# A two-layer diffusion trunk on one core: the first scale vector by column blocks, and the first two feed-forward products row tile by row tile

## The chip, the cores and the metric

The kernel runs on one core of a Trainium2 chip, as one program in one launch. The metric is the device time of that launch in microseconds (us). The core has five engines that run side by side, each through its own instructions in order: TensorE (matmuls; in the profile PE, and PEld for its weight loads), VectorE (DVE), ScalarE (ACT), GpSimd (POOL) and SyncE (SP), which here issues transfers. The transfers themselves run on 16 DMA engines.

## What is computed

Two layers of a backbone over 512 latent tokens and 256 context tokens of width 1024. Each layer is a half-step SwiGLU, a mixer, and a second half-step SwiGLU. Only the very start matters here: the modulation of layer 0 and the first feed-forward block.

```python
def adaln(cond, prm):
    mod = jax.nn.silu(cond) @ prm["mod_w"] + prm["mod_b"]
    return jnp.split(mod, N_MOD, axis=-1)
def half_ffn(x, m, name):
    sh, sc, g = m
    h = modulate(rms_norm(x, prm[name + "_norm"]), sh, sc)
    return x + 0.5 * g * swiglu(h, prm[name + "_w_in"], prm[name + "_w_out"])
```

The modulation is made for two conditions, one for the latent tokens and one for the context tokens. Of the nine chunks of 1024 entries, chunk 0 is the shift and chunk 1 the scale of the first feed-forward block.

## The kernel before

Tokens lie along the free axis: the input x is eight row tiles of 128 features by 768 tokens (`xv[d]`, tiles A, two to a buffer). The gain of the norm and the scale are multiplied to one factor per feature (`am`), the norm's reciprocal per token (`rb`) is applied behind the product, and the shift goes through the weights as extra columns. So the first products need `am` and x, but neither the norm nor the shift.

**A product** (`product(u)`) takes one unit of the input weights, 128 x 1024 values loaded by SP into a buffer `r` of two. ACT copies it in a rounded form (`wh`, L210) and DVE subtracts that from the original (`wl`, L211); tiles of x are split likewise into B (ACT, L386) and C (DVE, L387) by `prep(d)`. For each of the eight row tiles k three pairs of matmuls follow (`wh` with B, `wh` with C, `wl` with B), a pair being 512 and 256 tokens (helper line L190). Products are summed in PSUM in tiles `pa` (two) and `pb` (one). The first three products are "late" ones: the shift's columns come behind them, as 48 matmuls of 4 or 2 columns (`shifts`), once the shift is known.

**The scale and the shift** come from `mod_unit`: a unit is 128 rows of the modulation's weights by 1024 columns (512 KB), loaded by SP, and four fp32 matmuls of 256 columns in four strips of the array (L305; the trace counts each fp32 matmul as two). Eight units make a chunk, which two matmuls (L193) and DVE then bring into columns. At the start eight units run for the scale, through two buffers `m` and the two buffers `r`; a unit's load waits for the matmuls that used its buffer. Then SP loads the x tiles and the first two weight units, and `set_am` makes `am`. The eight units for the shift (`fill`) stand between the matmuls of products 1 and 2, one at every second row tile, through the two buffers `m`.

**Around it.** `sq_acc` squares the tiles of x on ACT (L374, L377) and sums them on POOL (L196); six matmuls with the sum as weights (L269, one column each), a chain on DVE and ACT, and two broadcast matmuls (L279) make `rb` during product 2 (`rb_steps`).

The order on each engine is set by a scheduler from the order of the code; instructions handed to `pin` keep their place. Buffers come from rings, and an instruction waits until the one that used its buffer last is done.

Of the kernel before, what the change touches and what calls it, by code (L numbers as in the profile page):

```python
# [8 lines left out]
F32 = mybir.dt.float32  # L9
F32R = mybir.dt.float32r  # L10
AF = mybir.ActivationFunctionType
ALU = mybir.AluOpType
# [7 lines left out]
NT = NL + NC  # L20
# [34 lines left out]
HD = 0  # L55
NLATE = 3
# [7 lines left out]
RAWD = (0, 5)  # L64
# [9 lines left out]
def _cols():  # L74
    if _COLS:
        return _COLS
    off = 0
    for name, n in (
        ("modb0", 72), ("modb1", 72), ("nrm0", 24), ("nrm1", 24), ("sel", 8),
        ("kvg", 2), ("qg", 3), ("gq96", 1), ("gk96", 1), ("glub", 8), ("dw", 124), ("dwb", 4),  # L80
        ("lng", 4), ("lnb", 4), ("gkr", 32), ("gqr", 32),
        ("gqq", 64), ("gqk", 64),
        ("ident", 128),
    ):
        _COLS[name] = (off, n)
        off += n
    _COLS["_n"] = (off, 0)
    return _COLS


class Kern:
    def __init__(self, tc, es, ins, out, dbg=None):
# [12 lines left out]
        const = pool("const", 1)  # L105
# [16 lines left out]
        nc.scalar.dma_start(self.small, ins["small"])  # L122
# [12 lines left out]
        nc.vector.tensor_copy(self.identr, self.col("ident"))  # L135
# [5 lines left out]
    def col(self, name):  # L141
        o, n = _cols()[name]
        return self.small[:, o:o + n]
# [149 lines left out]
    def mod_unit(self, both=False):  # L293
# [5 lines left out]
        if both and k % 2:  # L299
            u = self.wr.tile([128, 1024], F32, name=self.nm("r"), tag="r")  # L300
        else:
            u = self.mr.tile([128, 1024], F32, name=self.nm("m"), tag="m")
# [12 lines left out]
        for b in range(2):  # L315
# [4 lines left out]
                mb.unsqueeze(3).broadcast_to((128, 2, 4, 2)), ALU.add)  # L320

# [87 lines left out]
    def ffn(self, win, wout, lat_only, after, mid=None, late=None, fill=(), raws=(), split=None):  # L409
# [25 lines left out]
        def product(u):  # L435
            w = self.unit(win[u], 1024, self.pin if u < n_late else lambda i: i, raws.pop(0) if raws else None)
# [62 lines left out]
        u = j = 0  # L499
        for ci, n in enumerate(CHUNKS):  # L500
# [849 lines left out]
    def build(self):  # L1350
# [20 lines left out]
        for L in range(2):  # L1371
# [31 lines left out]
            first = dict(late=(lambda d: self.prep(d, False, self.pin), lambda d: self.sq_acc(d, NT, 0, self.pin), shift0), raws=raws, fill=[lambda: self.mod_unit(False)] * 8) if L == 0 else {}  # L1403
# [111 lines left out]
def layout(a):  # L1515
    a = {k: np.asarray(v) for k, v in a.items()}
    r = {}
# [6 lines left out]
    r["modw0"] = np.ascontiguousarray(a["l0_mod_w"][:, :2048])  # L1524
# [94 lines left out]
```

## Time and profile before

| what | before |
|---|---|
| median of three runs | 2865.4 us (2865.26 to 2869.09) |
| the profiled execution | 2866.9 us, of which the span is 2865.0 us |
| TensorE busy | 2792.8 us |
| VectorE, ScalarE, GpSimd busy | 1588.1, 858.3, 317.0 us |
| first product's first matmul | 22.87 us |
| first matmul behind the shift's columns | 72.85 us |

The page gives busy times by engine, and the chain of work that ended last, followed back from the end. The timeline shows each engine's instructions with start, duration and, in brackets, the idle time just before and what ended it; starts that follow each other closely are the better measure of a matmul's cost, since the durations overlap. The windows view gives busy time, the granted TensorE clock (1.00 is 2.4 GHz, 0.50 is 1.2 GHz) and the transfers' share in chosen stretches. The granted clock is printed as 1.00 until its first record, at 29.36 us here; before that the distance of the matmuls tells the pace.

### The profile page before, as it was taken

To read this page: it belongs to the slowest core of one execution; us is meant where nothing else is said; L and a number is where in the kernel's file an instruction comes from. 1 tells how busy PE (TensorE), PEld (TensorE's weight loads), DVE (VectorE), ACT (ScalarE), POOL (GpSimd) and SP (SyncE) were. 2 spreads that over 40 slices of the span, in tenths; PEclk is the share of its full clock that TensorE was granted. 3 is DMA by queue.
4 is the path that set the end of the run, shared out by engine and by line. 5 is a ranking of instruction groups with operands and counts; after the bars stand their busy time and mean duration, and the time that the engine had idled before them with its cause. 6 is when DMAs were issued, how large, how long until landed. Compare 5 with 4: busy or idle time off the path is not lost.

```text
span 2865.0 us, 41335 instructions
## 1 busy us (share of the span) xinstructions
PE 2792.8 (97%) x17180; PEld 2429.3 (85%) x17180; DVE 1588.1 (55%) x2618; ACT 858.3 (30%) x1284; POOL 317.0 (11%) x357
## 2 busy tenths in 40 slices
PE   7999999999978999999999999999999999999999
PEld 5888888887767788888888888888887878898998
DVE  2674675678565576747535432333347689644443
ACT  3221212242456422122122221221224267322222
POOL 1000000030022320000002100000021156300000
PEclk9999999999989999999999999999999999999999
DMA  6343343442200224426411121212133200322232
GB/s 234 126 149 109 116 156 104 133 138 75 72 30 20 63 95 130 151 89 208 160 66 60 60 67 59 66 54 69 61 101 114 60 12 31 96 92 93 90 102 89
DMA packets 80042, 272.22 MB, mean 95 GB/s; under 512 B 9456, under 2 KB 11248, under 8 KB 79728
## 3 DMA queue, kind: packets, MB, share of 16 engines
q1 hardware_dynamic: 72048, 252.11, 27.4%
q10 hardware_dynamic: 6144, 12.23, 1.4%
q0 software_dynamic: 1664, 5.24, 0.5%
q8 instruction: 136, 2.23, 0.3%
q14 instruction: 50, 0.41, 0.0%
HBM read 258.10 MB, written 7.34 MB: 93 GB/s over the span
## 4 chain that ended last, share of the span: by engine, by line
PE 64%; DVE 2%; ACT 1%; DMA 1%; issue 1%; POOL 0%; ACTq 0%; DVEq 0%; POOLq 0%
PE pa L190 39%; PE pb L190 19%; PE p L664 2%; PE pb L617 2%; DMA m<-in_modt 1%; PE pa L1229 1%; PE pa L1003 1%; ACT t L619 0%; DVE sm L630 0%; DVE m L339 0%; PE p L279 0%; PE pa L1255 0%; DVE wl L211 0%; PE p L1217 0%; ACT t L803 0%
## 5 line engine op out<-in xcount | busy, mean ns | idle before, releaser
L210 ACT CAST wh<-r 128x1024 fp32r<-128x1024 f32 (+3 forms) x334 | 341.7, 1023 | 1494.1 <-PE pa L190 778.4
L190 PE MATMUL pa<-B,wh 128*128 128x258 f32 (+2 forms) x1952 | 481.4, 328 | 2.7 <-ACT B L386 2.7
L190 PE MATMUL pa<-C,wh 128*128 128x258 f32 (+2 forms) x1952 | 481.7, 328 | 0.3 <-DVE C L387 0.3
L190 PE MATMUL pa<-B,wl 128*128 128x258 f32 (+2 forms) x1952 | 478.3, 326 | 0.0
L211 DVE TENSOR_TENSOR wl<-r,wh 128x1024 fp32r<-128x1024 f32 (+3 forms) x334 | 400.5, 1199 | 43.6 <-ACT wh L210 37.2
L190 PEld LDWEIGHTS pa<-B,wh 128*128 128x128 f32 x1952 | 303.6, 190 | 37.5 <-ACT B L386 2.7
L190 PEld LDWEIGHTS pa<-C,wh 128*128 128x128 f32 x1952 | 303.4, 190 | 35.0 <-issue 0.7
L190 PEld LDWEIGHTS pa<-B,wl 128*128 128x128 f32 x1952 | 303.6, 190 | 34.6
L190 PE MATMUL pa<-E,wh 128*128 128x512 f32 (+1 forms) x937 | 258.9, 345 | 1.8 <-POOL E L215 1.2
L190 PE MATMUL pb<-B,wh 128*128 128x512 f32 (+1 forms) x992 | 244.3, 327 | 0.0
L190 PE MATMUL pb<-C,wh 128*128 128x512 f32 (+1 forms) x992 | 243.4, 327 | 0.0
L190 PE MATMUL pb<-B,wl 128*128 128x512 f32 (+1 forms) x992 | 242.7, 326 | 0.0
L475 DVE COPY sm<-pa 128x2 f32<-128x2 f32 x115 | 18.2, 158 | 403.2 <-PE pa L190 403.2
L190 PE MATMUL pa<-D,wh 128*128 128x512 f32 (+1 forms) x800 | 207.0, 337 | 0.7 <-ACT D L227 0.6
L190 PE MATMUL pa<-D,wl 128*128 128x256 f32 (+1 forms) x752 | 200.1, 339 | 0.0
L339 DVE SCALAR_TENSOR_TENSOR m<-m,cb 128x1024 f32<-128x1024 f32 x128 | 157.1, 1230 | 28.9 <-DMA m<-in_modt 28.3
L190 PEld LDWEIGHTS pa<-E,wh 128*128 128x128 f32 x937 | 150.2, 188 | 24.8 <-POOL E L215 1.6
L190 PEld LDWEIGHTS pb<-B,wl 128*128 128x128 f32 x992 | 153.9, 190 | 17.9 <-issue 0.5
L190 PEld LDWEIGHTS pb<-B,wh 128*128 128x128 f32 x992 | 153.7, 189 | 17.8 <-issue 1.5
L190 PEld LDWEIGHTS pb<-C,wh 128*128 128x128 f32 x992 | 153.4, 189 | 17.1 <-issue 0.2
L190 PEld LDWEIGHTS pa<-D,wh 128*128 128x128 f32 x800 | 125.4, 188 | 19.9 <-ACT D L227 0.9
L199 DVE SCALAR_TENSOR_TENSOR A<-pa,hg,A 128x256 f32<-128x256 f32 (+1 forms) x96 | 55.3, 613 | 144.8 <-PE pa L190 144.8
(328 smaller groups left out, 4197.7 us busy)
## 6 DMA issues: line engine op xcount, KB each, us to landing
m<-in_modt SPq DMA_DIRECT2D x128, 512.0 KB, 4.2
r<-in_win0a SPq DMA_DIRECT2D x44, 512.0 KB, 3.5
r<-in_win0b SPq DMA_DIRECT2D x44, 512.0 KB, 3.5
r<-in_win1a SPq DMA_DIRECT2D x44, 512.0 KB, 3.4
r<-in_win1b SPq DMA_DIRECT2D x44, 512.0 KB, 3.4
r<-in_wodd SPq DMA_DIRECT2D x18, 512.0 KB, 3.8
r<-in_wout0a SPq DMA_DIRECT2D x20, 448.0 KB, 3.9
r<-in_wout1a SPq DMA_DIRECT2D x20, 448.0 KB, 3.3
```

What stands on the lines that cost most here:

```text
L190: self.nc.tensor.matmul(out, l.bitcast(F32R), r.bitcast(F32R), start=st, stop=sp)
L199: self.nc.vector.scalar_tensor_tensor(o, a, s, b, op0=op0, op1=op1)
L210: pin(self.nc.scalar.copy(hi, r))
L211: pin(self.nc.vector.tensor_tensor(lo, r, hi.bitcast(F32), op=ALU.subtract))
L339: nc.vector.scalar_tensor_tensor(o, u, 1.0, self.cb[:, v * 1024:(v + 1) * 1024], op0=ALU.mult, op1=ALU.mult, accum_out=self.mod[L][:, f, v ...
L475: nc.vector.tensor_copy(w2[:, o:o + 2], p[:, so:so + 2])
L617: pin(nc.tensor.transpose(pt[:, ks], P[:, ks], self.col("ident")))
L664: self.pin(self.nc.tensor.matmul(self.po[i * 64:(i + 1) * 64, col:col + 128], v, self.PTs[i][:, kt * 128:(kt + 1) * 128], start=(kt == 0), ...
L1003: self.pin(nc.tensor.matmul(s[:, o:o + b - a], q[:, ts].bitcast(F32R), k[:, a:b].bitcast(F32R), start=j == 0, stop=j == 2))
L1229: self.pin(nc.tensor.matmul(s[:, a:b], q.bitcast(F32R), k[:, a:b].bitcast(F32R), start=j == 0, stop=j == 1))
```

## The change

The scale is no longer computed chunk by chunk of its input, but by its output: a column block d is all 1024 input rows by the 128 outputs that row tile d needs, and is stored so that it loads as one 128 x 1024 tile (`modp`, 512 KB). `mod_col(f, u)` takes such a block as weights, in eight fp32 matmuls with two columns, and two small DVE operations make the eighth part of `am`. SP loads column block and row tile in turn, with the two first weight units behind the first pair. `head()` then runs products 0 and 1 together: per row tile the scaling, six pairs of matmuls, the squares. The column blocks use the two buffers `m` (blocks 0, 1, 4, 5) and the two buffers `r` (2, 3, 6, 7, behind the first two weight units). All eight units for the shift now lie in product 2, one at each row tile. The first 96 columns of the small vectors are loaded apart (`small0`).

```diff
-    def mod_unit(self, both=False):
+    def mod_unit(self):
...
-        if both and k % 2:
-            u = self.wr.tile([128, 1024], F32, name=self.nm("r"), tag="r")
-        else:
-            u = self.mr.tile([128, 1024], F32, name=self.nm("m"), tag="m")
+        u = self.mt()
...
+    def mod_col(self, f, u):
+        p = self.p1()[:, 0:2]
+        for k in range(8):
+            self.pin(self.nc.tensor.matmul(p, u[:, k * 128:(k + 1) * 128], self.sT[:, k, 0:2], start=k == 0, stop=k == 7))
+        o = self.mod[0][:, 8 + f, :]
+        self.pin(self.nc.vector.tensor_scalar(o, p, self.col("modb0")[:, 8 + f:9 + f], None, op0=ALU.add))
+        self.pin(self.nc.vector.tensor_scalar(self.am[:, f, :], o, 1.0, self.col("nrm0")[:, f:f + 1], op0=ALU.add, op1=ALU.mult))
...
             for k in range(8):
-                if u == 0 and late:
-                    late[0](k)
                 ks = slice(k * 128, (k + 1) * 128)
...
-                if u and fill and k % 2:
+                if u and fill:
                     fill.pop(0)()
-                if u == 1 and late:
-                    late[1](k)
...
+        def head():
+            ws = [self.unit(win[u], 1024, self.pin, raws[u]) for u in range(2)]
+            for u in range(2):
+                kept.append((u, ws[u]))
+                pt[u] = self.pd()
+            for k in range(8):
+                late[0](k)
+                ks = slice(k * 128, (k + 1) * 128)
+                for u in range(2):
+                    for i, (l, x) in enumerate(three(ws[u], (xh, xl))):
+                        for a, b, o in (grp[0], (512, 768, 512)):
+                            self.mm(pt[u][:, o:o + b - a], l[:, ks], x[k][:, a:b], k == 0 and i == 0, k == 7 and i == 2)
+                late[1](k)
...
-        self.mq = [(L, m) for L in range(2) for m in order]
+        self.mq = [(L, m) for L in range(2) for m in order][1:]
         self.xv = self.rows("A", NT)
-        for _ in range(8):
-            self.mod_unit(True)
-        raws = []
+        raws, cols = [], []
+        ring = lambda: self.wr.tile([128, 1024], F32, name=self.nm("r"), tag="r")
         for d in range(8):
+            cols.append(ring() if d in (2, 3, 6, 7) else self.mt())
+            nc.sync.dma_start(cols[d], I["modp"][d])
             nc.sync.dma_start(self.xv[d], I["xT"][:, d, :])
-            if d in RAWD:
-                raws.append(self.raw(I["win0a"][len(raws)], 1024))
-        self.set_am(0, 0, 1)
+            if d == 0:
+                raws += [self.raw(I["win0a"][u], 1024) for u in range(2)]
...
+        def first0(d):
+            if d == 0:
+                self.mod_col(0, cols[0])
+            self.prep(d, False, self.pin)
+            if d < 7:
+                self.mod_col(d + 1, cols[d + 1])
```

How the order changes shows best on TensorE. Its first instructions before, with the units of the scale chunk (`m`, `r`), the two matmuls that bring it into columns, and the first product (`pa`):

```order
L305 MATMUL p_115<-m_116,cb_88 32x256 x4
L305 MATMUL p_115<-r_122,cb_88 32x256 x4
L305 MATMUL p_115<-m_128,cb_88 32x256 x4
L305 MATMUL p_115<-r_134,cb_88 32x256 x4
L305 MATMUL p_115<-m_140,cb_88 32x256 x4
L305 MATMUL p_115<-r_146,cb_88 32x256 x4
L305 MATMUL p_115<-m_152,cb_88 32x256 x4
L305 MATMUL p_115<-r_158,cb_88 32x256 x4
L193 MATMUL p_166<-small,t_164 128x8 x2
L190 MATMUL pa_203<-B_19_183,wh_199 128x512
```

And its first instructions now, with column products (L323) and the first row tile's pairs for products 0 (`pa_161`) and 1 (`pa_162`):

```order
L323 MATMUL p_163<-cb_88,m_115 128x2 x8
L323 MATMUL p_178<-cb_88,m_122 128x2 x8
L190 MATMUL pa_161<-B_16_145,wh_153 128x512
L190 MATMUL pa_161<-B_16_145,wh_153 128x256
L190 MATMUL pa_162<-B_16_145,wh_157 128x512
L190 MATMUL pa_161<-C_20_149,wh_153 128x512
...
L190 MATMUL pa_162<-B_16_145,wl_158 128x256
L323 MATMUL p_206<-cb_88,r_125 128x2 x8
L190 MATMUL pa_161<-B_16_145,wh_153 128x512
```

Two column products stand ahead of the first row tile's matmuls, and one more ahead of each further tile's.

On SP, the issues before, at the end of the scale chunk's units: x follows, with the weight units among it (the names are those of the buffers).

```order
L303 DMA m_152<-in_modw 128x1024
L303 DMA r_158<-in_modw 128x1024
L1361 DMA A_2_111<-in_xT 128x768
L203 DMA r_171<-in_win0a 128x1024
L1361 DMA A_2_111<-in_xT 128x768
L1361 DMA A_3_112<-in_xT 128x768 x2
```

And now, from the first issue on:

```order
L119 DMA cb_88<-in_cT 128x256
L1381 DMA m_115<-in_modp 128x1024
L1382 DMA A_2_111<-in_xT 128x768
L203 DMA r_118<-in_win0a 128x1024
L203 DMA r_120<-in_win0a 128x1024
L1381 DMA m_122<-in_modp 128x1024
L1382 DMA A_2_111<-in_xT 128x768
L1381 DMA r_125<-in_modp 128x1024
L1382 DMA A_3_112<-in_xT 128x768
```

Column block and row tile now alternate, and the first two weight units stand behind the first pair.

In product 2 on TensorE (`pb`), before, behind the row sums (L269): a unit of the shift chunk (L305) after six pairs.

```order
L269 MATMUL p_397<-ones,acc 128x1 x6
L190 MATMUL pb_390<-B_19_183,wh_386 128x512
...
L190 MATMUL pb_390<-C_23_187,wh_386 128x256
L190 MATMUL pb_390<-B_19_183,wl_387 128x512
L190 MATMUL pb_390<-B_19_183,wl_387 128x256
L305 MATMUL p_302<-m_410,cb_88 32x256 x4
L190 MATMUL pb_390<-B_20_184,wh_386 128x512
```

And now the same place, with the units at L302:

```order
L190 MATMUL pb_415<-C_20_149,wh_411 128x512
L190 MATMUL pb_415<-C_20_149,wh_411 128x256
L302 MATMUL p_422<-m_423,cb_88 32x256 x4
L190 MATMUL pb_415<-B_16_145,wl_412 128x512
L190 MATMUL pb_415<-B_16_145,wl_412 128x256
L269 MATMUL p_429<-ones,acc 128x1 x6
...
L190 MATMUL pb_415<-B_16_145,wl_412 128x256
L302 MATMUL p_422<-m_442,cb_88 32x256 x4
L190 MATMUL pb_415<-B_17_146,wh_411 128x512
```

Where a unit stood at every second row tile of products 1 and 2, one stands at every row tile of product 2.

## Rows read from the trace of the kernel before

**Rows 1.** The page: busy time by engine, and the chain that ended last.

```profile
PE 2792.8 (97%) x17180; PEld 2429.3 (85%) x17180; DVE 1588.1 (55%) x2618; ACT 858.3 (30%) x1284; POOL 317.0 (11%) x357
PE 64%; DVE 2%; ACT 1%; DMA 1%; issue 1%; POOL 0%; ACTq 0%; DVEq 0%; POOLq 0%
```

**Rows 2.** Timeline, TensorE, 6 to 26 us: start, duration, instruction, idle before and releaser.

```profile
6.29 1.08 PE L305 MATMUL p<-m,cb 128*32 128x256 f32 x8 [6.29 <-DMA m<-in_modw]
...
10.22 1.08 PE L305 MATMUL p<-r,cb 128*32 128x256 f32 x8 [0.20 <-DMA r<-in_modw]
...
22.87 1.01 PE L190 MATMUL pa<-B,wh 128*128 128x512 f32 x2 [2.65 <-ACT B L386]
...
24.98 0.84 PE L190 MATMUL pa<-B,wl 128*128 128x512 f32 x2
25.62 0.84 PE L190 MATMUL pa<-B,wh 128*128 128x512 f32 x2
```

**Rows 3.** Timeline, TensorE, 29 to 50 us: products 0 to 2, shift units, row sums.

```profile
29.77 0.52 PE L190 MATMUL pa<-C,wh 128*128 128x512 f32 x2
...
33.98 0.40 PE L190 MATMUL pa<-C,wh 128*128 128x512 f32 x1
...
40.52 0.64 PE L305 MATMUL p<-m,cb 128*32 128x256 f32 x8
41.09 0.62 PE L190 MATMUL pa<-B,wh 128*128 128x512 f32 x2
...
43.40 0.64 PE L305 MATMUL p<-m,cb 128*32 128x256 f32 x8
...
46.84 0.62 PE L190 MATMUL pb<-B,wh 128*128 128x512 f32 x2
...
47.98 1.39 PE L269 MATMUL p<-ones,acc 128*128 128x1 f32 x12
49.24 0.61 PE L190 MATMUL pb<-B,wh 128*128 128x512 f32 x2
```

**Rows 4.** Timeline, TensorE, 60 to 73 us: last shift unit, shift matmuls, next product.

```profile
60.38 0.64 PE L305 MATMUL p<-m,cb 128*32 128x256 f32 x8
...
63.01 0.27 PE L190 MATMUL pa<-xs,wh 128*128 128x4 f32 x1 [0.69 <-DVE xs L196]
...
63.68 0.35 PE L190 MATMUL pa<-xs,wl 128*128 128x2 f32 x1
...
72.64 0.35 PE L190 MATMUL pb<-xs,wl 128*128 128x2 f32 x1
72.85 0.99 PE L190 MATMUL pa<-B,wh 128*128 128x512 f32 x2
```

**Rows 5.** Timelines of ACT and of DVE, 20 to 32 us.

```profile
21.15 1.04 ACT L210 CAST wh<-r 128x1024 fp32r<-128x1024 f32 x1 [16.94 <-DMA r<-in_win0a]
22.10 8.33 ACT L386 ACTIVATE B<-A,am 128x512 fp32r<-128x512 f32 x16
...
20.26 0.17 DVE L196 TENSOR_TENSOR mod<-p,small 128x16 f32<-128x16 f32 x1 [1.12 <-PE p L193]
...
22.23 1.23 DVE L211 TENSOR_TENSOR wl<-r,wh 128x1024 fp32r<-128x1024 f32 x1 [1.58 <-ACT wh L210]
23.37 8.55 DVE L387 SCALAR_TENSOR_TENSOR C<-A,am,B 128x512 fp32r<-128x512 f32 x16
```

**Rows 6.** DMA view, 33 to 62 us: issues, KB each, median us to landing.

```profile
m<-in_modw SPq DMA_DIRECT2D x6, 512.0 KB, 3.7
```

**Rows 7.** Windows view: busy us (instructions) by engine, granted clock, DMA share, GB/s.

```profile
63.50:72.80 9.30, 9.30 (x45) 9.30 (x46) 3.63 (x12) 4.37 (x5) 0.00 (x0) 0.50 0.34 136
72.80:77.10 4.30, 4.30 (x14) 3.72 (x15) 4.07 (x7) 3.08 (x4) 0.00 (x0) 0.50 0.64 205
...
947.60:950.90 3.30, 3.30 (x26) 2.97 (x23) 0.28 (x1) 1.08 (x3) 0.70 (x1) 0.50 0.00 0
```

More of the change, by code (lines that the diff above doesn't have):

```diff
@@ L55 @@
 HD = 0
+FIRST = 96
 NLATE = 3
@@ L63 @@
 NQA = ()
-RAWD = (0, 5)
 BA = 1
@@ L78, in _cols @@
     for name, n in (
-        ("modb0", 72), ("modb1", 72), ("nrm0", 24), ("nrm1", 24), ("sel", 8),
+        ("modb0", 72), ("nrm0", 24), ("modb1", 72), ("nrm1", 24), ("sel", 8),
         ("kvg", 2), ("qg", 3), ("gq96", 1), ("gk96", 1), ("glub", 8), ("dw", 124), ("dwb", 4),
@@ L121, in __init__ @@
         self.small = const.tile([128, cols["_n"][0]], F32, name="small")
-        nc.scalar.dma_start(self.small, ins["small"])
+        self.small0 = const.tile([128, FIRST], F32, name="small0")
+        nc.scalar.dma_start(self.small0, ins["small"][:, :FIRST])
         self.sl = pool("sl", 1)
@@ L134, in __init__ @@
         self.identr = const.tile([128, 128], F32R, name="identr")
-        nc.vector.tensor_copy(self.identr, self.col("ident"))
         self.gcomb = const.tile([128, 1], F32, name="gcomb")
@@ L142, in col @@
         o, n = _cols()[name]
-        return self.small[:, o:o + n]
+        return self.small0[:, o:o + n] if o < FIRST else self.small[:, o:o + n]
     def nm(self, p):
@@ L435, in product @@
         def product(u):
-            w = self.unit(win[u], 1024, self.pin if u < n_late else lambda i: i, raws.pop(0) if raws else None)
+            w = self.unit(win[u], 1024, self.pin if u < n_late else lambda i: i)
             if not late:
@@ L499, in ffn @@
         u = j = 0
+        if late:
+            head()
+            u = 2
         for ci, n in enumerate(CHUNKS):
@@ L1354, in build @@
         order = (1, 0, 2, 4, 3, 5, 7, 6, 8)
-        self.mq = [(L, m) for L in range(2) for m in order]
+        self.mq = [(L, m) for L in range(2) for m in order][1:]
         self.xv = self.rows("A", NT)
-        for _ in range(8):
-            self.mod_unit(True)
-        raws = []
+        raws, cols = [], []
+        ring = lambda: self.wr.tile([128, 1024], F32, name=self.nm("r"), tag="r")
         for d in range(8):
+            cols.append(ring() if d in (2, 3, 6, 7) else self.mt())
+            nc.sync.dma_start(cols[d], I["modp"][d])
             nc.sync.dma_start(self.xv[d], I["xT"][:, d, :])
-            if d in RAWD:
-                raws.append(self.raw(I["win0a"][len(raws)], 1024))
-        self.set_am(0, 0, 1)
+            if d == 0:
+                raws += [self.raw(I["win0a"][u], 1024) for u in range(2)]
+        nc.scalar.dma_start(self.small[:, FIRST:], I["small"][:, FIRST:])
+        nc.vector.tensor_copy(self.identr, self.col("ident"))
         self.prep_rows(False)
+        def first0(d):
[4 more added lines that the diff above has]
+                self.mod_col(d + 1, cols[d + 1])
         def shift0():
@@ L1401, in ready @@
                 self.set_am(L, 1, 4)
-            first = dict(late=(lambda d: self.prep(d, False, self.pin), lambda d: self.sq_acc(d, NT, 0, self.pin), shift0), raws=raws, fill=[lambda: self.mod_unit(False)] * 8) if L == 0 else {}
+            first = dict(late=(first0, lambda d: self.sq_acc(d, NT, 0, self.pin), shift0), raws=raws, fill=[self.mod_unit] * 8) if L == 0 else {}
             self.ffn(I[f"win{L}a"], I[f"wout{L}a"], False, spill, {0: lambda: gate(2), 2: ready}, split=halves, **first)
@@ L1523, in layout @@
     r["cT"] = cT
-    r["modw0"] = np.ascontiguousarray(a["l0_mod_w"][:, :2048])
+    r["modw0"] = np.ascontiguousarray(a["l0_mod_w"][:, :1024])
+    r["modp"] = np.ascontiguousarray(a["l0_mod_w"][:, 1024:2048].reshape(8, 128, 8, 128).transpose(2, 1, 0, 3).reshape(8, 128, 1024))
     r["cB"] = np.ascontiguousarray(np.broadcast_to(np.concatenate([a["c"][0], a["c_ctx"]]), (128, 2048)))
```

## The prediction

> **What bounds the kernel now.** I read the page's summary first: TensorE is busy for 97% of the span and holds 64% of the chain that ended last [rows 1]. So a microsecond saved or lost on TensorE before the first steady product moves the end by about a microsecond, and nothing off TensorE counts unless TensorE waits for it. Then I read TensorE's timeline of the first 77 us, the whole region that the change touches. Four pieces follow one another. Until 22.87 us TensorE does little: the eight row blocks of the scale chunk land (the first at 6.29 us, the next three at about 1.3 us each), their eight units of matmuls run, and only then can the first row tile be scaled; the idle time before the first product ends on ACT's B [rows 2]. From 22.87 to 46.84 us products 0 and 1 run, from 46.84 us product 2, with the eight units of the shift chunk between their matmuls; the last of these starts at 60.38 us and takes 0.6 us, so this piece ends at 61.0 us [rows 3, 4]. From 63.01 to 72.85 us stand 48 tiny shift matmuls, and from 72.85 us on the products run steadily [rows 4]. The change rebuilds all that lies ahead of 61.0 us. From the shift's matmuls on, the order of TensorE, ACT, DVE and POOL is the same in both kernels, so I ask one thing: when does the last unit of the shift chunk end, against 61.0 us now.
>
> Two paces must be told apart. A pair of matmuls of 512 and 256 columns starts every 0.64 us from 24.98 us on, which is 1.2 GHz, and every 0.35 us from 29.77 us on (12 pairs in 4.21 us), which is 2.4 GHz [rows 2, 3]. Matmuls of one column, which are all weight load, stand 0.11 us apart at the upper level (12 from 47.98 us, nearly 1.3 us), those of 2 and 4 columns 0.213 us at the lower (42 in 8.96 us) [rows 3, 4].
>
> **Removed, and added ahead of the first product.** The wait for all eight blocks of the scale chunk goes. The first tile now needs one column block, one row tile and two weight units. The first block lands at 6.3 us as now; behind it, at 1.3 us for 512 KB and so about 1.0 for 384 KB, come the row tile at 7.3, the two weight units at 8.6 and 9.9 and the second column block at 11.2 us [rows 2]. ACT casts both units (1.04 us each) until 10.9 us. DVE subtracts both (1.23 us each) until 12.2 us, and only behind them stand its two small operations for the first block (0.2 us each), until 12.6 us; then ACT scales the tile (16 instructions in 8.33 us now, so 1.04 a tile) until 13.7 and DVE makes its low part (8.55 us for eight) until 14.3 us [rows 5]. TensorE meanwhile has the second column product in front of the first tile: 8 fp32 matmuls, which the trace counts as 16 (the 6 of the row sums stand there as 12 [rows 3]), at 0.213 us are 3.4 us, from 11.2 to 14.6 us. So the first tile starts at 14.6 us, 8.3 us before today.
>
> **Added between the tiles.** Each of the eight tiles brings a column product of 16 weight loads. At the upper level that is 16 x 0.111 = 1.8 us, at the lower 3.4 us, and nothing hides it: it stands on TensorE, in order, between the tiles. Changing kind costs too: a unit of today holds TensorE for 0.57 us (40.52 to 41.09), but from one unit to the next, 2.88 us (40.52 to 43.40), there are six pairs of 0.351, so it costs 0.77 [rows 3]. I put that 0.2 us on a column product: 2.0 us. A tile of two products is six pairs: 2.11 us at the upper level, 3.84 us at the lower. No other engine is near that: per tile ACT has 1.04 us of scaling and one square, DVE 1.5 us, and the transfers 2.3 us, with four column buffers; TensorE is the bound. If the clock rises during the first tile's products (my likeliest case), that tile ends at about 18.4 us, six column products take 12.0 and seven tiles 14.8 us: products 0 and 1 end at 45.2 us, against 46.84. Of the 8.3 us, 1.6 are left.
>
> **Moved into product 2.** Today four units of the shift chunk lie ahead of 46.84 us and four in product 2, which takes 14.1 us with them (46.84 to 61.0) [rows 3, 4]; now all eight lie there, one each eighth. Without any wait that is 14.1 + 4 x 0.77 = 17.2 us. But the units have two buffers and land 3.7 us after their issue [rows 6], and unit n+2 is issued when unit n is done. Counted from the start of product 2 in the order's sequence: unit 2 is done at 4.9 us; unit 4 lands at 8.7 and is done at 9.3; unit 6 has landed when its place comes at 14.0, and is done at 14.6; unit 8 lands at 18.3 and is done at 18.9 us. So 4.8 us are lost. Bounds: 3.1 us if no transfer is waited for, 7.2 if each of three lands 0.8 us later beside the weight units in the same queue (an estimate). I take 4.8, since the 3.7 us are of the same tile in the same stage.
>
> The Trainium skill (DMA: Bandwidth & Descriptors, section Anatomy of one DMA) gives about 2.0 us plus the bytes at 436 GB/s, which would be 3.2 us for such a unit, as an estimate; the trace has 3.7. By the page's figure about 0.5 us less would be lost.
>
> **Edits with one answer.** The small vectors' split into two loads adds one issue on ACT's queue at the start, ahead of nothing late; DVE's cast of the identity, which waits for the second part, ends long before the weight units land. The sum of squares now follows each tile and its last tile reaches POOL about a microsecond before product 2 starts, so the row sums 1.6 us into it are just covered; if not, that costs some tenths. The 48 shift matmuls stay, at the lower level as now (0.50 over 63.5 to 72.8 us) [rows 7].
>
> **Sum.** -1.6 + 4.8 = +3.2 us. The profiled execution took 2866.9 us, so by it 2870.1; against the median of the three runs, 2865.4, it is 2868.6 us, which I give. A measurement tells 0.2%, 5.7 us, from no change.
>
> **Rivals.** *The clock rises late (slower).* The products of the opening are no longer one dense stretch, but bursts of 3.84 us with 3.4 us of tiny matmuls between. Tiny ones do not lift the clock: over 9.3 us of them, back to back, the granted clock stayed at 0.50, and it rose 4.3 us after dense matmuls had begun [rows 7]. At the start it took about 6 us of products before the pace changed [rows 2, 3]; at 947.6 us a dense stretch of 3.3 us was enough [rows 7]. A burst of 3.84 us lies between these: the clock may rise in the first or in a later one. Each further tile at the lower level costs 1.7 us of products and 1.4 to 1.6 us of column product, so 3.3: one gives 2871.9, two 2875.2, three 2878.5 us. If it never rises in the head, products 0 and 1 end at 14.6 + 8 x 3.84 + 6 x 3.4 = 65.7 us, 20.5 late, near 2889 us. The rival decides from the point where the third tile starts at the lower level. Once up the clock should stay, since 12 tiny matmuls inside product 2 are followed by products at full pace [rows 3].
>
> The Trainium skill (TensorE: Matmul & The Clock Gate, section HAM oscillation — how this bites in real kernels) describes a loop whose short bursts are parted by waits for transfers and which starts each at the lower clock. By that rule the head would stay at 1.2 GHz: the 2889 us of this rival. No row here shows bursts parted by tiny matmuls, and I give it 5 in 100.
>
> *TensorE follows the inputs (faster).* If a column product cost TensorE next to nothing, because its weight loads ran under the products, the head would be set by transfers: the second row tile is in at 12.2 us, six more blocks and tiles at 2.3 us are 26 us, and with the last tile's scaling and products, near 5 us, the head ends at 31: 14 us less than 45.2, near 2854 us. Against it: the row sums load weights of the same shape and stand 0.11 us apart, with the next product behind them only [rows 3]. It counts as faster from column products under 1.0 us. *The transfers of product 2 are hidden:* the sum is -1.6 + 3.1, 2866.9 us.
>
> **How the numbers follow.** Clock up in the first tile, sum as above or with the transfers hidden: 51 (of it 5 over the 5.7 us by small waits). One tile late: 14, half of it over 5.7 us. Two or more late: 15. Never: 5. Column products or transfers much cheaper, or a first tile well before 14.6 us: 15, of which 13 go below 5.7 us. So faster 0.13, slower 0.32, the same 0.55. The likeliest case alone holds 2865 to 2871. The range leaves out the head that never warms, the far end of the faster case and a clock over three tiles late: 2860 to 2878 us.
>
> **What would show it.** Right: the first pair near 14.6 us; column products of about 2 us between tiles; product 2 starting near 45 us; TensorE waits of about a microsecond for m near its end; the last unit done near 64 us. Wrong: pairs 0.64 us apart beyond 22 us (late clock), TensorE waiting for column blocks or row tiles between tiles (transfers), or product 2 starting before 39 us.

## The result, and the profile after

The changed kernel takes 2872.3 us (median of 13 runs, 2868.7 to 2882.3) beside 2866.4 us of the kernel before, measured with it (13 runs). The ratio is 1.0023, with a 95% interval of 1.0014 to 1.0032, which is 4.0 to 9.2 us. So the change makes the kernel slower by about 6 us: the forecast had the sign, and its 2868.6 us lies 3.7 us under the measured time, but its +3.2 us lies below the interval.

The profiled execution after took 2872.5 us, of which the span is 2870.7 us, against 2865.0 before. From the page of after, the busy time, to be held against [rows 1]:

```profile
PE 2802.9 (98%) x17240; PEld 2446.1 (85%) x17240; DVE 1591.5 (55%) x2631; ACT 859.0 (30%) x1284; POOL 316.4 (11%) x357
```

TensorE is busy for 10.1 us more, now 98% of the span. The page can't say where; the timeline of TensorE from 4 to 24 us can (start, duration, instruction, idle before and releaser), to be held against [rows 2]:

```profile
6.32 3.54 PE L323 MATMUL p<-cb,m 128*128 128x2 f32 x16 [6.32 <-DMA m<-in_modp]
11.18 3.57 PE L323 MATMUL p<-cb,m 128*128 128x2 f32 x16 [1.32 <-DMA m<-in_modp]
14.61 1.41 PE L190 MATMUL pa<-B,wh 128*128 128x512 f32 x3
...
17.32 0.58 PE L190 MATMUL pa<-C,wh 128*128 128x512 f32 x2
17.73 0.51 PE L190 MATMUL pa<-B,wl 128*128 128x512 f32 x2
18.08 1.84 PE L323 MATMUL p<-cb,r 128*128 128x2 f32 x16
19.78 0.60 PE L190 MATMUL pa<-B,wh 128*128 128x512 f32 x2
...
21.99 1.84 PE L323 MATMUL p<-cb,r 128*128 128x2 f32 x16
```

The two first column products run at the lower level (3.5 us), the first tile starts at 14.61 us, and from about 17.4 us the pairs stand 0.35 us apart: the clock rose inside the first tile's burst. From then on a tile costs 3.91 us (18.08 to 21.99), of which the column product has 1.70 (18.08 to 19.78). TensorE waits for nothing between tiles. The next stretch, product 2 with all eight shift units, is what [rows 3] and [rows 4] show of before:

```profile
44.00 0.51 PE L190 MATMUL pb<-B,wh 128*128 128x512 f32 x2
...
44.79 0.64 PE L302 MATMUL p<-m,cb 128*32 128x256 f32 x8
45.91 0.62 PE L190 MATMUL pb<-B,wl 128*128 128x512 f32 x2 [0.48 <-DVE wl L211]
46.36 1.40 PE L269 MATMUL p<-ones,acc 128*128 128x1 f32 x12
...
49.37 1.08 PE L302 MATMUL p<-m,cb 128*32 128x256 f32 x8
...
55.11 0.64 PE L302 MATMUL p<-m,cb 128*32 128x256 f32 x8
...
60.38 0.64 PE L302 MATMUL p<-m,cb 128*32 128x256 f32 x8
...
62.89 0.64 PE L302 MATMUL p<-m,cb 128*32 128x256 f32 x8 [0.97 <-DMA m<-in_modw]
64.61 0.64 PE L302 MATMUL p<-m,cb 128*32 128x256 f32 x8 [1.09 <-DMA m<-in_modw]
...
67.64 0.37 PE L190 MATMUL pa<-xs,wh 128*128 128x4 f32 x1 [0.69 <-DVE xs L196]
...
77.90 0.99 PE L190 MATMUL pa<-B,wh 128*128 128x512 f32 x2
```

Product 2 starts at 44.00 us, 2.84 earlier than before, and the last unit ends at 65.25 (64.61 + 0.64), 4.23 later than before (60.38 + 0.64 = 61.02). So the piece that took 14.2 us takes 21.2. Its order is not quite one unit at each row tile: the scheduler has put the third unit behind eleven and a half of the 24 pairs, and the last two behind all of them. At the first steady product the kernel is 5.05 us late (77.90 against 72.85), which is nearly all of the 5.7 us between the spans. Two things in this piece are new: TensorE waits for the shift's units, and the clock falls. The windows view (busy us of PE, PEld, DVE, ACT and POOL, granted clock, transfers' share, GB/s):

```profile
44.00:48.00 4.00, 3.52 (x30) 2.66 (x29) 2.02 (x2) 1.02 (x2) 0.77 (x1) 1.00 0.39 126
48.00:52.00 4.00, 4.00 (x20) 2.42 (x19) 1.65 (x5) 0.20 (x1) 0.00 (x0) 0.57 0.13 30
52.00:56.00 4.00, 4.00 (x29) 2.02 (x28) 0.00 (x0) 0.58 (x1) 0.00 (x0) 1.00 0.90 331
```

The 0.48 us for `wl` have a cause of their own. The timelines of POOL and of DVE at that place:

```profile
42.92 1.85 POOL L196 TENSOR_TENSOR acc<-acc,t 128x768 f32<-128x768 f32 x1 [2.49 <-ACT t L383]
```

```profile
43.75 2.10 DVE L211 TENSOR_TENSOR wl<-r,wh 128x1024 fp32r<-128x1024 f32 x1 [0.92 <-ACT wh L210]
```

DVE's subtraction, 1.23 us elsewhere [rows 5], takes 2.10 while POOL adds the last square until 44.77.

### The profile page after: what moved, and what is told of

Same layout as the page of the kernel before. It is cut to its first block, busy times and chain, and to the rows that moved or that the text cites. A ratio compares the mean times of both kernels' runs of the same rounds, so it can differ in the third digit from the quotient of the medians.

```text
span 2870.7 us, 41474 instructions
## 1 busy us (share of the span) xinstructions
PE 2802.9 (98%) x17240; PEld 2446.1 (85%) x17240; DVE 1591.5 (55%) x2631; ACT 859.0 (30%) x1284; POOL 316.4 (11%) x357
## 4 chain that ended last, share of the span: by engine, by line
PE 63%; DVE 3%; ACT 1%; DMA 1%; issue 1%; POOL 1%; ACTq 0%; DVEq 0%; POOLq 0%
PE pa L190 39%; PE pb L190 19%; PE p L684 2%; PE pb L637 1%; DMA m<-in_modt 1%; PE pa L1249 1%; PE pa L1023 1%; DVE sm L650 0%; ACT t L639 0%; DVE m L345 0%; POOL t L645 0%; PE p L279 0%; PE pa L1275 0%; DVE wl L211 0%; PE p L1237 0%
## 5 line engine op out<-in xcount | busy, mean ns | idle before, releaser
L492 DVE COPY sm<-pa 128x2 f32<-128x2 f32 x115 | 18.3, 159 | 403.2 <-PE pa L190 403.2
```

Of the source, the lines that this page charges most:

```text
L492: nc.vector.tensor_copy(w2[:, o:o + 2], p[:, so:so + 2])
```

## The experiments

Two theories stood. **The buffers:** product 2 is long since eight units go through two buffers, and each load waits for a unit before it. **The clock:** it is long since the clock falls inside it. Behind them stands the question of what bounds the head.

**Four buffers for the shift units.** Each second unit is loaded into the ring `r`, as the scale's units were before the change.

```diff
-        u = self.mt()
+        u = self.wr.tile([128, 1024], F32, name=self.nm("r"), tag="r") if k % 2 else self.mt()
```

> The changed kernel, but the eight shift units go through four buffers (m and r in turn) where they went through two. Theory A (the loss sits in product 2, where each unit's load waits for the unit two before it): the two waits for m near the end of product 2 (0.97 and 1.09 us) go, product 2 with its units takes 17 to 18 us where it took 21.2, and the kernel is 3 to 4 us faster than the changed one, near the kernel before. Theory B (the loss is the column products' 1.8 us each, which the change puts on TensorE; the waits only fill time that would be lost anyway): at most 1 us faster than the changed one.

Measured: 2865.9 us (12 runs) beside 2864.9 of before (23 runs), ratio 1.0007 with an interval of 0.9997 to 1.0017, which can't be told from the kernel before. TensorE's timeline, the start of product 2, the last unit and the first shift matmul:

```profile
45.83 0.51 PE L190 MATMUL pb<-B,wh 128*128 128x512 f32 x2
...
62.32 0.64 PE L302 MATMUL p<-r,cb 128*32 128x256 f32 x8
...
64.94 0.27 PE L190 MATMUL pa<-xs,wh 128*128 128x4 f32 x1 [0.69 <-DVE xs L196]
```

No unit is waited for. The piece takes 17.1 us (45.83 to 62.96), which is the prediction's sum without any wait, 14.1 + 4 x 0.77 = 17.2. The clock fell here too, but from 42.2 to 45.6 us, still in the head. With the two ratios held against each other (1.0023 and 1.0007), the buffers are worth some 4.6 us, give or take 4 by the two intervals. That is theory A, and the greater part of the loss.

**One of the eight matmuls of a column product.** This takes TensorE's column work away and asks what bounds the head then.

```diff
-        for k in range(8):
-            self.pin(self.nc.tensor.matmul(p, u[:, k * 128:(k + 1) * 128], self.sT[:, k, 0:2], start=k == 0, stop=k == 7))
+        self.pin(self.nc.tensor.matmul(p, u[:, 0:128], self.sT[:, 0, 0:2], start=True, stop=True))
```

> The changed kernel with one matmul of the eight in each column product, so the scale is summed over an eighth of its inputs: the transfers, the waits and the order around them stay. Theory B: six column products between tiles fall from about 1.95 to 0.4 us, product 2 starts 6 to 9 us earlier than at 44.0 us and the kernel is 6 to 9 us faster than the changed one, so faster than the kernel before. Theory A: the head becomes bound by the scaling chain or the transfers, product 2 starts at most 3 us earlier, and the time stays within 3 us of the changed kernel.

Measured: 2865.1 us (11 runs), ratio 1.0003 (0.9994 to 1.0011). Product 2 starts at 41.05 us, only 3.0 earlier, although some 1.5 us per tile were gone: the tiles still follow each other every 3.89 us. That is theory A; the ratios would put this kernel 5.7 us under the changed one, where theory A had at most 3, but in the trace the first steady product comes only 2.3 us earlier (75.60 against 77.90). The timeline of all engines in one tile:

```profile
28.29 1.83 POOL L196 TENSOR_TENSOR acc<-acc,t 128x768 f32<-128x768 f32 x1 [2.06 <-ACT t L382]
28.35 1.79 DVE L325 TENSOR_SCALAR am<-mod,small 128x2 f32<-128x2 f32 x1
30.17 1.12 ACT L391 ACTIVATE B<-A,am 128x512 fp32r<-128x512 f32 x2 [2.03 <-DVE am L325]
...
30.95 0.96 PE L190 MATMUL pa<-B,wh 128*128 128x512 f32 x4 [1.31 <-ACT B L391]
```

DVE's operation on two columns, 0.23 us in the changed kernel, begins just after POOL's add begins and ends when that does (30.14 and 30.12). A ring of four operations sets the pace: the scale, B, the square, the add, and only then the next scale. The Trainium skill (SBUF — State Buffer, section SBUF: two separate sides) says that GpSimd shares one pair of SBUF ports with those VectorE operations that run in a two-port mode or take two inputs from SBUF, and that the one that starts first keeps the pair for its whole instruction. By that rule the small operation, if it is one of these, would last as long as the add, and the trace agrees: 1.79 us instead of 0.23.

**The same, with the additions on DVE.** This tests that ring.

```diff
-            self.tt(acc, acc, t, ALU.add, self.nc.gpsimd)
+            self.tt(acc, acc, t, ALU.add, self.nc.vector if pin == self.pin else self.nc.gpsimd)
```

> As the run with one of eight matmuls per column product (seven eighths of the scale's inputs left out), with the opening's seven additions of squares (128x768) on VectorE instead of GpSimd. Theory A (VectorE's scale operation L325 is held for as long as GpSimd adds, and this chain of scale, B, square and add sets the pace of 3.89 us per tile): the scale operation falls from 1.8 to about 0.23 us, the pace falls to 2.5 to 2.9 us per tile, product 2 starts at 32 to 35 us instead of 41.05, and the span is 5 to 8 us shorter than the 2863.1 us of that run (2855 to 2858). Theory B (the scale operation waits for its PSUM read or for TensorE, whoever adds): it stays at 1.7 to 1.8 us, and the pace at 3.9 us or more since VectorE has 0.95 us more per tile; product 2 at 41 us or later, span 2863 to 2868.

Measured: one execution of 2862.4 us, span 2860.7. DVE and TensorE in a tile:

```profile
28.60 0.97 PE L190 MATMUL pa<-B,wh 128*128 128x512 f32 x4 [0.49 <-ACT B L391]
29.77 0.95 DVE L196 TENSOR_TENSOR acc<-acc,t 128x768 f32<-128x768 f32 x1
30.64 0.22 DVE L325 TENSOR_SCALAR am<-mod,small 128x2 f32<-128x2 f32 x1
```

The scale operation is back at 0.22 us, so the hold was POOL's add. The pace falls to 3.07 us (28.60 to 31.67), product 2 starts at 38.20, and the span is 2.4 us shorter. Each is a smaller gain than was expected (2.5 to 2.9, 32 to 35, and 5 to 8 us): the scheduler put the add ahead of the scale operation, so the ring still turns through it, with 0.95 us in place of 1.83.

**Column blocks alone, products 0 and 1 one after the other.** The products and the shift units are as before the change, only the scale comes by column blocks (the core of the edit).

```diff
             for k in range(8):
+                if u == 0 and late:
+                    late[0](k)
...
-                if u and fill:
+                if u and fill and k % 2:
                     fill.pop(0)()
+                if u == 1 and late:
+                    late[1](k)
...
-        if late:
-            head()
-            u = 2
```

> Column blocks alone: the scale by column blocks and the tiles as they arrive, as in the changed kernel, but products 0 and 1 one after the other and the shift units at every second row tile of products 1 and 2, as before. Theory A: the units' loads are hidden again, the last unit ends near 61 us as in the kernel before, and the time is within 1.5 us of the kernel before, 4 to 6 us under the changed one. Theory B: the column products cost the same here, so the time stays near the changed kernel, 2870 to 2873 us.

Measured: 2887.5 us (5 runs), ratio 1.0076 (1.0064 to 1.0088), far beyond what either theory had. TensorE's timeline:

```profile
24.13 0.84 PE L190 MATMUL pa<-B,wl 128*128 128x512 f32 x2
24.90 3.58 PE L323 MATMUL p<-cb,r 128*128 128x2 f32 x16
29.81 0.80 PE L190 MATMUL pa<-B,wh 128*128 128x512 f32 x1 [1.33 <-ACT B L392]
...
60.14 0.95 PE L302 MATMUL p<-m,cb 128*32 128x256 f32 x2
61.02 0.61 PE L190 MATMUL pa<-B,wl 128*128 128x512 f32 x2
```

The pairs stand 0.64 us apart and the column products last 3.4 to 3.6 us until 60.8 us. With only three pairs per tile, parted by column products at 1.2 GHz and twice by a wait of 1.33 us for B, the clock did not rise in all of product 0; it rose in product 1, where no column products part the pairs. This is the rival of the late clock at its far end, in a head with half the burst; the prediction had put it near 2889 us for the changed kernel. The Trainium skill (TensorE: Matmul & The Clock Gate, section HAM oscillation — how this bites in real kernels) has such a loop, with waits for transfers between short bursts that each start at the lower clock; here tiny matmuls fill the pauses, and the trace shows the same.

**The order of the head alone.** The scale comes by eight row units as before, products 0 and 1 run together, all eight shift units lie in product 2.

```diff
-            cols.append(ring() if d in (2, 3, 6, 7) else self.mt())
-            nc.sync.dma_start(cols[d], I["modp"][d])
...
+        for _ in range(8):
+            self.mod_unit(True)
...
+        self.set_am(0, 0, 1)
```

> The other half alone: the scale by eight row units as before the change, but products 0 and 1 together tile by tile and all eight shift units in product 2. Theory A: first product at 22.9 us as before, product 2 starts near 44 us, takes 19 to 21 us with its units, and the last unit ends 2 to 4 us later than in the kernel before: 2868 to 2871 us. Theory B: without column products nothing is lost, and the time is within 1 us of the kernel before.

Measured: 2874.4 us (5 runs), ratio 1.0033 (1.0020 to 1.0046), above what either theory had. TensorE's timeline:

```profile
25.27 1.44 PE L190 MATMUL pa<-B,wh 128*128 128x512 f32 x3 [4.21 <-ACT B L392]
...
36.84 0.39 PE L190 MATMUL pa<-C,wh 128*128 128x256 f32 x1 [1.47 <-DVE C L393]
...
69.10 0.64 PE L302 MATMUL p<-m,cb 128*32 128x256 f32 x8 [1.98 <-DMA m<-in_modw]
```

Three losses add up. The first tile waits until both weight units are cast (25.27 us instead of 22.87). DVE's C, now beside POOL's adds, takes up to 2.35 us where it took up to 0.75, and TensorE waits for it twice (1.47 and 1.46 us). So product 2 starts at 49.58 us, 2.7 later than before, and running the products together gains nothing here by itself. The largest loss is product 2: its units are waited for as in the changed kernel, and it takes 20.2 us (49.58 to 69.74) where it took 14.2, with no column block in the kernel.

**Row sums one eighth later.** In the first trace of the changed kernel the clock falls just behind the 12 tiny matmuls of the row sums, which stand beside the first unit and the wait for `wl`. Here they move away from both.

```diff
-        rb = rb[:1] + [None] * RBW + rb[1:]
+        rb = [None] * bool(late) + rb[:1] + [None] * RBW + rb[1:]
```

> The changed kernel with one edit: the six small matmuls of the row sums (L269) stand one eighth later in product 2, so that they no longer lie beside the first shift unit and the 0.48 us wait for the cast weights. Theory A (the clock fell at 48.17 us because the unit, the wait and the tiny row sums lay together without a product between them): no stretch of 1.2 GHz in 44 to 52 us, product 2 shorter by about 1.5 us (3.41 us at the lower level, of which a little under half is lost), last unit ends near 63.7, median 2870.5 to 2871. Theory B (the fall belongs to something earlier, since it also stood at 42.2 with four buffers and at 45.1 with the shortened column products): a stretch of some 3.4 us at 1.2 GHz is still there between 40 and 52 us, last unit near 65.2, median 2872 to 2873.

Measured: 2869.7 us (10 runs) beside 2863.7 of before (25 runs), ratio 1.0021 (1.0012 to 1.0031), so no gain that can be told over the changed kernel's 1.0023. The fall was gone, but this execution had another misfortune, in a head that is the changed kernel's own:

```profile
25.09 0.84 PE L190 MATMUL pa<-B,wl 128*128 128x512 f32 x2
25.73 2.24 PE L323 MATMUL p<-cb,r 128*128 128x2 f32 x16
```

The clock rose only at 26.6 us, behind the second tile, and product 2 started at 48.14. The same instructions had the rise at 17.4 us before. To tell the edit from chance, both kernels ran again unaltered.

> The changed kernel once more, unaltered, for the granted clock alone. In its first trace the clock rose at 17.45 us in the first tile's burst and fell from 48.17 to 51.58 us in product 2; with the row sums one eighth later it rose at 26.56 us and didn't fall before 67.5. Theory A (the order of the instructions sets both): rise at 16 to 19 us, product 2 at 44 us, a stretch at 1.2 GHz that begins within 47 to 50 us. Theory B (where a rise or a fall comes is partly a matter of the single execution): the rise comes up to 10 us later, or the fall is elsewhere or missing, and product 2 starts anywhere from 44 to 49 us; the shift matmuls then stand between 66 and 71 us.

> The changed kernel a third time, with the same two theories as the run before it: theory A the same rise (16 to 19 us) and the same fall (beginning within 47 to 50 us); theory B another pair, with product 2 between 44 and 49 us.

> The kernel with the row sums one eighth later, unaltered, once more. Theory A (the later row sums take the fall out of product 2): no stretch at 1.2 GHz between the rise and the end of product 2, whenever the rise comes. Theory B (chance of the single execution): a fall between 40 and 55 us in this one. Its head is the changed kernel's, so a rise at 17 us and product 2 at 44 us here would say that the late rise of its first trace was not the edit's doing.

Single times were 2869.7, 2872.8 and 2870.3 us. With the traces from before, times in us; rise and fall from the trace's record of the granted clock, the piece is from product 2's start to the last unit's end:

| execution | clock up at | low again | product 2 starts | last unit ends | piece | waits for m | shift matmuls start |
|---|---|---|---|---|---|---|---|
| changed, first | 17.4 | 48.2 to 51.6 | 44.00 | 65.25 | 21.2 | 2.06 | 67.64 |
| changed, second | 18.6 | 49.3 to 52.8 | 44.73 | 67.19 | 22.5 | 2.97 | 69.57 |
| changed, third | 19.0 | 42.9 to 46.3 | 46.38 | 66.42 | 20.0 | 2.90 | 68.81 |
| sums later, first | 26.6 | none before 67.5 | 48.14 | 69.08 | 20.9 | 2.87 | 71.47 |
| sums later, second | 19.5 | none before 63.9 | 45.02 | 66.00 | 21.0 | 2.90 | 68.40 |
| four buffers | 18.3 | 42.2 to 45.6 | 45.83 | 62.96 | 17.1 | none | 64.94 |

The falls, in windows of the second and of the third execution of the changed kernel:

```profile
49.50:52.50 3.00, 3.00 (x15) 1.76 (x14) 1.19 (x3) 0.00 (x0) 0.00 (x0) 0.50 0.20 40
```

```profile
43.00:46.00 3.00, 3.00 (x11) 2.59 (x10) 2.08 (x3) 2.93 (x3) 1.83 (x1) 0.50 0.42 147
```

Theory B holds for the rise: it differs between executions of the same head by up to 9 us. The Trainium skill (TensorE: Matmul & The Clock Gate, section What's actually happening) says that the moment of the rise varies from run to run, by plus or minus half a microsecond, since the monitor runs free of the kernel's start. The table agrees that it varies, but by more: 17.4 to 19.5 us in four executions of this head, 26.6 in the fifth. For the fall the table leaves two readings. All three executions of the changed kernel had one before 60 us and neither with the later sums did, but one of the three lies in the head, ahead of the row sums, and so does that with four buffers. What triggers it stays open. What it costs in the piece can be read in part: without a fall between 44 and 60 us the piece takes 20.0 us in the changed kernel (third execution) and 20.9 and 21.0 with the sums later, where the last unit runs at 1.2 GHz; with a fall inside it 21.2 and 22.5. Where TensorE is not slowed, it waits, as here in the third execution of the changed kernel:

```profile
62.82 0.64 PE L302 MATMUL p<-m,cb 128*32 128x256 f32 x8 [0.58 <-DMA m<-in_modw]
65.78 0.64 PE L302 MATMUL p<-m,cb 128*32 128x256 f32 x8 [2.32 <-DMA m<-in_modw]
```

So the two buffers set most of the length of the piece: 20.0 us in it without a fall, 17.1 with four buffers. Up to the sixth unit the executions can be told apart: it is done 15.0 us after the start of product 2 in the third execution, which has neither a fall nor the wait for `wl`, 15.5 with the sums later, which has the wait (0.5 us) and no fall, and 17.0 in the first two, which have both. So a fall inside the piece costs some 1.5 us, and it is handed on to the last unit. Where the fall lies in the head, or the rise comes late, the time is lost ahead of product 2.

**A cheaper column product.** From the above: four buffers, sums later, additions on DVE, and the column product turned round. The vectors are now the weights (32 columns, four strips at once) and the block moves, 128 columns at a time; DVE copies the strips out, one matmul against a two-column selector adds them, and the strips run two tiles ahead.

```diff
-        for k in range(8):
-            self.pin(self.nc.tensor.matmul(p, u[:, k * 128:(k + 1) * 128], self.sT[:, k, 0:2], start=k == 0, stop=k == 7))
...
+        for h in range(2):
+            for c in range(4):
+                k = 4 * h + c
+                self.pin(self.nc.tensor.matmul(p[32 * c:32 * c + 32, 0:128], self.sT[:, k, :], u[:, k * 128:(k + 1) * 128],
+                                               start=h == 0, stop=h == 1, tile_position=(0, 32 * c)))
+        t = self.t768()[:, :128]
+        self.pin(self.nc.vector.tensor_copy(t, p[:, 0:128]))
...
+        self.pin(self.nc.tensor.matmul(o, t, self.col("sel2"), start=True, stop=True))
+        self.pin(self.nc.vector.tensor_scalar(self.am[:, f, :], o, self.b1[:, f:f + 1], self.col("nrm0")[:, f:f + 1], op0=ALU.add, op1=ALU.mult))
```

> Four buffers for the shift units, row sums one eighth later, additions of squares on VectorE, and the column product turned round: per block eight matmuls with 32 columns of the vectors as weights and 128 columns of the block moving, four at a time in four strips, a copy of the strips to SBUF by VectorE, and one matmul against a two-column selector that adds the strips; the strips run two tiles ahead. Theory A (the head is bound by TensorE's column products, 1.84 us per tile at 2.4 GHz, and, once these are short, by VectorE held by GpSimd): column work falls to about 0.6 us per tile, pace 2.6 to 2.9 us per tile, product 2 starts near 36 us (44.0 changed, 46.84 before), the shift matmuls near 57 us (63.0 before, 67.6 changed), median 2857 to 2861. Theory B (with shorter work between the waits the clock stays at 1.2 GHz in the head as it did to 60.8 us with the products one after the other): pace about 4.5 us per tile, product 2 near 50 us, median 2868 to 2874. Theory C (the inputs bound the head as soon as TensorE is relieved): waits for blocks or row tiles show ahead of the strips, product 2 at 38 to 42 us, median 2861 to 2865.

Measured: 2857.4 us (10 runs) beside 2863.7, ratio 0.9982 (0.9972 to 0.9991): 6.3 us faster than the kernel before, 2.6 to 8.0 by the interval. Four buffers alone had 1.0007. TensorE's timeline, one tile's column work, then the marks of product 2 and the shift:

```profile
22.78 0.28 PE L334 MATMUL p<-small,t 128*128 128x2 f32 x2
22.99 0.64 PE L325 MATMUL p<-m,cb 128*32 128x128 f32 x16
23.56 0.61 PE L190 MATMUL pa<-B,wh 128*128 128x512 f32 x2
...
39.95 0.52 PE L190 MATMUL pb<-B,wh 128*128 128x512 f32 x2
...
56.46 0.64 PE L302 MATMUL p<-r,cb 128*32 128x256 f32 x8
...
59.01 0.27 PE L190 MATMUL pa<-xs,wh 128*128 128x4 f32 x1 [0.69 <-DVE xs L196]
```

Column work is 0.78 us per tile (22.78 to 23.56) instead of 1.70, the pace 3.0 us (22.99 to 25.96) instead of 3.9, with no wait of TensorE between tiles. The piece of product 2 takes 17.15 us (39.95 to 57.10), as with four buffers alone, and the shift matmuls start 4.0 us earlier than before the change. Theory A had the mechanism; its sizes were 2 us too hopeful at the shift (57 forecast) and 4 at product 2.

**The same with the additions on POOL.**

```diff
-            self.tt(acc, acc, t, ALU.add, self.nc.vector if pin == self.pin else self.nc.gpsimd)
+            self.tt(acc, acc, t, ALU.add, self.nc.gpsimd)
```

> The same kernel with the additions of squares left on GpSimd. Theory A (GpSimd's add holds VectorE's small scale operation and its subtractions): scale operations of 1 to 1.8 us in most tiles, pace 3.3 to 3.9 us per tile, product 2 at 41 to 45 us, median 5 to 8 us above that of the kernel with the additions on VectorE (2864 to 2867). Theory B (the hold only shows where VectorE has nothing else to do): the scale operation runs before the add starts, pace 2.6 to 2.9, product 2 near 36 us, median within 2 us of the other kernel's.

Measured: 2859.7 us (10 runs), ratio 0.9986 (0.9977 to 0.9996). The median is 2.3 us above that of the run before and the intervals of the two overlap, so theory A's 5 to 8 us fell. The opening is no slower: product 2 starts at 38.45 us and the shift matmuls at 58.26, both earlier than with the additions on DVE, so the 2.3 us arise later, if at all. POOL and DVE in a tile, and at the weight unit of product 2:

```profile
24.44 1.83 POOL L196 TENSOR_TENSOR acc<-acc,t 128x768 f32<-128x768 f32 x1 [1.16 <-ACT t L392]
25.09 0.28 DVE L335 TENSOR_SCALAR am<-p,sm,small 128x2 f32<-128x2 f32 x1 [0.74 <-PE p L334]
```

```profile
37.47 2.10 DVE L211 TENSOR_TENSOR wl<-r,wh 128x1024 fp32r<-128x1024 f32 x1 [0.93 <-ACT wh L210]
```

The scale operation runs in the middle of POOL's add and is not held. It differs from the held one in that it takes its tensor from PSUM (`p`), not from SBUF (`mod`). Its start in the middle of the add is not what frees it: in the run with one of eight matmuls a scale operation from SBUF that started at 17.83 us, inside an add from 16.60 to 18.42, ended at 18.44 as well. The subtraction from SBUF is held here as in the changed kernel (2.10 us). Theory B's reason, that the operation runs before the add, is not what happened either. So the earlier opening did not need the additions on DVE.

## Why the prediction was right, and where its size was off

The sum was -1.6 for the head, +4.8 for product 2 and nothing behind it: +3.2 us. In the profiled execution it is -2.84, +7.07 (21.25 against 14.18) and +0.82 (from the last unit's end to the first steady product 12.65 against 11.83 us): +5.05 at 77.90 us. The rest of the spans' 5.7 us arises later; short stretches of lower clock lie there, which differ between executions of the changed kernel. So the head, 1.2 us better than forecast, hid half of the 2.3 us by which product 2 was worse. By its own chances the outcome was not the likeliest one: it gave 0.55 to a change within 5.7 us and 0.32 to a slower one, and the medians lie 5.9 us apart, with an interval (4.0 to 9.2) on both sides of that line.

- **The first tile** was to start at 14.6 us; it started at 14.61. The chain of landings, casts and two column products at the lower level was right.
- **The clock in the first tile's burst** was the likeliest case, and three of the five executions of this head show it (17.4, 18.6 and, at the burst's end, 19.0 us); in a fourth the clock rose in the column product behind that burst (19.5), with no further tile at the lower level. One shows the rival, a tile late, with product 2 starting 3.1 to 4.1 us later than in the three others whose head has no fall; 3.3 per tile was forecast. The far end of that rival is real as well, in a head with half the burst (blocks alone, 2887.5 us).
- **The column product** was put at 2.0 us and costs 1.70. Of the 0.2 us for changing kind, taken from the shift units, half shows, in the six pairs behind it: 2.21 us (19.78 to 21.99) instead of 2.11. So a tile costs 3.91 us instead of 4.1, and the head ended 1.2 us earlier than forecast, at 44.00.
- **Product 2 is the term that was mis-sized:** 18.9 us forecast, 21.2 measured, 20.0 to 22.5 over five executions, the far bound being 21.3. The part without waits was exact (17.2 against 17.1 with four buffers), and the walk through two buffers had the mechanism. It had units 2, 4, 6 and 8 done at 4.9, 9.3, 14.6 and 18.9 us from the start of product 2. In the profiled execution they were done at 6.5, 11.8, 17.0 and 21.2, and each delay is handed on, since a unit's load is issued only when the unit two before it is done. The third execution of the changed kernel, which has neither the 0.48 us wait for `wl` nor a fall of the clock in this piece, has 4.9, 9.7, 15.0 and 20.0. So up to unit 6 the walk was right within 0.4 us, and 2.0 us more came from the wait (0.5) and the clock (1.5), which it did not have. The last load is the other part: the median of six is as assumed (beside 3.7 us in [rows 6]), and the last of the profiled execution took 3.5 us, but in the four other executions the last unit started 4.3 to 4.5 us after its load's issue. That is the 0.8 us of the far bound; a weight unit beside it is not what makes it, for the load of unit 4, with one issued 0.4 us behind it, took 3.7. The Trainium skill's 3.2 us, which the prediction sets beside the 3.7 and which that section gives for transfers issued by GpSimd, was not met: the six of the profiled execution, issued by SP, took 3.4 to 4.5 us. The DMA view of after, 43 to 67 us (issues, KB each, median us to landing), and that of the third execution, 61 to 62 us, with the last unit's load alone:

```profile
m<-in_modw SPq DMA_DIRECT2D x6, 512.0 KB, 3.6
```

```profile
m<-in_modw SPq DMA_DIRECT2D x1, 512.0 KB, 4.3
```

- **"Once up the clock should stay"** failed: it fell in all three executions of the changed kernel. That the twelve row sums of before were followed by products at full pace was too little to conclude from.
- **The row sums** were just covered, as forecast. What was overlooked is that the cover itself, POOL's last add, holds DVE's subtraction.
- **"TensorE is the bound"** was right for this kernel but not by the margin claimed. "No other engine is near that" is refuted: with the column products nearly free, the ring through DVE and POOL ran at 3.89 us per tile, as much as TensorE's 3.91. For the same reason the rival *TensorE follows the inputs* could not have come true at its price: with the scale operation as it is, neither column work nor transfers decide below about 3.9 us per tile. With the other form of the operation the pace was 3.0.
- **Behind product 2** nothing was forecast, and 0.8 us came: the clock is down from 65.2 us, ahead of the shift's last steps, where before it fell at 63.5, after the first shift matmuls.

## What to carry to other kernels

Work that is moved from a stage with idle buffers into one with few is priced by the slowest chain of buffer, load and user, and every delay ahead of a user lengthens that chain; giving the moved loads back the second pair of buffers was worth more than the whole gain of the head (some 4.6 against 2.8 us). A product with two useful columns is cheaper with the vectors as weights, in strips, than with the matrix as weights: here 0.78 against 1.70 us of TensorE per block, the adding up included, at the price of one copy on DVE. When one engine is relieved, look for a ring through the others that has the same period already.

## What the runs showed of the hardware that was not expected

GpSimd's add over 128x768 (1.83 us) holds a VectorE operation on two columns for its whole length (1.79 instead of 0.23 us) and stretches a 128x1024 subtraction from 1.23 to 2.10 us, but not the operation on two columns that takes its tensor from PSUM (0.28 us in the middle of an add). The moment at which TensorE's clock rises under the same head differed by 9 us between executions, and with bursts of three pairs between column products it stayed at the lower level until 60.8 us.
